# Inverse of the first and last recurrence in one piece, products of r behind it

## The chip, the cores and the metric

The kernel runs on one core of a Trainium2 chip. Its time is device microseconds of one execution; runs are compared by their medians. TensorE (PE) multiplies into PSUM, VectorE (DVE), ScalarE (ACT) and GpSimd (POOL) do the elementwise work, and SyncE (SP) issues the loads.

## The reference, cut to what matters

Two blocks follow each other, all in fp32 on 256 tokens of 1024 features. The first block has two layers over two streams, x and a context ctx. Each layer projects a stream, runs a convolution of 31 taps on one half and a recurrence (RWKV-7 like) on the other, mixes them, and adds a gated FFN:

```python
def step(s, inp):                       # per token, head and direction
    r_t, k_t, v_t, w_t, kk_t, b_t = inp
    sa = -jnp.einsum("bhvk,bhk->bhv", s, kk_t)
    s = s * w_t + sa[..., None] * b_t + v_t[..., None] * k_t   # shapes cut
    y = jnp.einsum("bhvk,bhk->bhv", s, r_t) if emit else None
    return s, y
...
z = val * jax.nn.sigmoid(gate)          # the convolution beside it
z = dwconv(z, conv_w) + conv_b          # 31 taps
z = silu(group_norm(z, CONV_GROUPS, cnorm_g, cnorm_b, LN_EPS))
...
mod_x = silu_c @ ada_w[l] + ada_b[l]    # adaLN: six vectors of 1024 per layer and stream
```

There are 8 heads of 64 and two directions. The second block (FFN, gated mixer, FFN, twice) isn't touched by the change.

## The kernel before, in words

**Recurrences.** `rwkv` (L763) does one stream in chunks of 64 tokens. It makes decays, learning rates and keys, then for each of four pairs of heads the tiles AR (a and r) and BK (k and b), and the 64x64 lower triangles of products of a and b (L862 to L864). `inverse` (L941) inverts these triangles: a transpose on VectorE (L950), 31 steps of two dependent VectorE instructions each (L959, L961: a product of 31-k by k+1 elements, and a subtraction), then two more transposes (L964, L966), matmuls of 32x32 and copies into the tiles Q. It is a generator that is left once behind the 31 steps, so the code emitted there stands between the steps and the rest of the inverse. `reads` (L1011) makes, for one pair of heads, the masked products of r with k and b (VectorE mask L1026), and token-major k and b (transposes L1032, ScalarE copies L1033). `values` (L1038) makes, for two pairs, token-major v (transposes L1049, copies L1051) and the masked products of a and k with it (mask L1062). `chain` (L1072) then goes through the chunks, for two groups of two pairs side by side: a product with Q, the state product (L1104), and the output products.

It runs four times: ctx of layer 0 and x of layer 1 in mode "wide", x of layer 0 in mode "half", and ctx of layer 1 in mode "all". The two wide ones are the first and the last recurrence; in the trace they begin their inverse at 110.0 and 1200.6 us. "half" does reads and values between the chains, "all" without r products.

**What runs beside a wide recurrence.** `wide` (L1402) hands `rwkv` a `fill` that emits steps of other work between the chains' steps: the convolution's input product `conv_in` (L657: eight weight tiles, each loaded, copied to an upper part by ScalarE at L339, its lower part made by VectorE at L340, then 24 matmuls; a product with a sigmoid on VectorE at L668), and then the adaLN vectors 2 to 5 (`ada_steps`, L476: unsplit weight tiles against the conditioning, a small VectorE add at L501). Behind the recurrence it emits the convolution's taps (`conv`, L698: on VectorE at L723, on GpSimd at L729 and L730, a few products on ScalarE at L727).

**What sets the order.** All loops are unrolled. A planner takes the instructions with their dependencies and puts each engine's in a fixed order, by a time line that it simulates: of what is ready, the one that was emitted first goes first; `later(n)` lets what it holds give way to n instructions behind it (the last tiles of the recurrence's own input product, v and gate, are such). Whatever is ready can go into a pause of earlier work. `tc.issue_after(ins)` ties what is emitted inside, on the engine of `ins`, behind `ins` in that engine's order; it adds no wait for its end.

**Shared space.** Tiles of one tag are handed out in program order. In a wide recurrence `reads` and `values` share two PSUM banks, acc10 and acc11 (lane "t"), which one chain group uses later; the input products and adaLN share two banks "pb" (lane "b"); the weight loads four tiles "raw". The token-major v tiles (L1043) come from the tag "xf", whose four tiles hold the normalised input of the block until its last reader, the convolution's input product, is done.

Of the kernel before, what the change touches and what calls it, by code (L numbers as in the profile page):

```python
# [21 lines left out]
ALPHA = 4.0 ** 0.25  # L22
# [5 lines left out]
# weight stream: buffers of raw tiles, of their upper and lower parts, and those the second block adds; the tiles after  # L28
# a norm that are split ahead of it
# [3 lines left out]
# steps of a down product that are cut by tokens at its end, in the first block and in the second  # L33
NLAST = 2, 4
# taps of the convolution on Pool, and on Pool with the products on ACT: first wide stream, second, beside the FFN
NPOOL, NPOOLE, NPOOLC = (14, 3), (12, 4), (30, 0)
NTAP = 2
# adaLN vectors: with the first wide recurrence, with the second, in the first FFN (a step every EVERY tiles)
QB, QE, QC, EVERY = (2, 3, 4, 5), (2, 3, 4, 5), (1,), 2
# steps of the filler per step of the recurrence's chain; instructions that low-priority work gives way to  # L40
FILL = 6
LATER = 1500
# slots of 4 KB in the first block; its norms with the weight tiles behind them held back
# [4 lines left out]
# ---------------------------------------------------------------- host layout  # L48
# [58 lines left out]
# the constants of the first norm  # L107
NCONST1 = CONST["tri0"][0]
LEVELS = (64, 32, 16, 8, 4, 2, 1)
# order of the RWKV column tiles in the weight stream: decay|iclr, k, r, v, gate  # L110
# [3 lines left out]
def _constants():  # L114
# [33 lines left out]
    # level indicators: [b0 level 128 | 64 | 32 | ... | 1 | b1 level 128]  # L148
# [10 lines left out]
    # hindT rows 0..3 for the four heads of 128  # L159
# [6 lines left out]
def _layout(a):  # L166
    f = {}
# [39 lines left out]
    for l in range(2):  # L207
# [27 lines left out]
        f[f"mf{l}"] = (_up(np.concatenate([w[:, 512:1024], w[:, :512]], 1)))  # zf, zq  # L235
        f[f"mt{l}"] = (np.concatenate(
            [w[:, o : o + 512].reshape(4, 2, P, 512).transpose(0, 2, 1, 3).reshape(4, P, D) for o in (1024, 2560)], 0))
        f[f"mg{l}"] = (_up(np.concatenate([w[:, 1536:2048], w[:, 2048:2560]], 1)))  # zg, zu
# [8 lines left out]
# ---------------------------------------------------------------- the program  # L247
# [9 lines left out]
class Prog:  # L257
# [17 lines left out]
    # Tiles of one tag are handed out in program order, so work that runs side by side has tags of its own:  # L275
    # lane "r" (the recurrences), "b" (the large products), "c" (the convolution).
# [33 lines left out]
    @contextlib.contextmanager  # L310
    def later(self, n):
        """what is emitted inside gives way to the n instructions behind it"""
        self.tc.cur_priority += n
        yield
        self.tc.cur_priority -= n

# [25 lines left out]
    # ---- weight stream: tiles of [128, 1024]  # L342
# [6 lines left out]
    def wsplit(self, r):  # L349
        """(hi, lo)"""  # L350
# [7 lines left out]
        if not self.hold:  # L358
            self.split(r, hi, lo)
        elif self.since < NFIRST:  # L360
            # ready ahead of the norm before the product, out of the way of it
            self.nc.scalar.copy(hi, r)  # L362
            self.nc.gpsimd.tensor_sub(lo, r, hi.bitcast(F32))  # L363
        else:
            with self.tc.issue_after(self.hold[0]), self.tc.issue_after(self.hold[1]):
                self.split(r, hi, lo)
            if self.since > NFIRST + 3:
                self.hold, self.since = None, 0
# [7 lines left out]
    # ---- norms  # L376
    def rstd_of(self, ssum, scale, eps, shape):
        """1 / sqrt(ssum * scale + eps)"""
# [7 lines left out]
    def ln_norm(self, x, b, pre):  # L386
        """pre(b, h): what makes half h of the block"""
# [19 lines left out]
    def rms_blocks(self, blocks, keep=False):  # L407
        """the two blocks [128, 1024] of tokens normalised, with keep in place"""
# [17 lines left out]
    def feature_major(self, yb, scale, bias, perm=False, new=None, acc=True):  # L426
        """the two blocks [128, 1024] of tokens, times scale(f) plus bias(f) -> list of 8 (hi, lo) [128, 256]"""
# [4 lines left out]
        # in the banks of the product before, or else two features at a time  # L432
# [4 lines left out]
        # evacuated by ACT and DVE in turns of two, as the products take them; each engine in the order given here  # L437
# [33 lines left out]
    # ---- adaLN  # L471
# [4 lines left out]
    def ada_steps(self, l, qs):  # L476
        """a generator of a quarter of a modulation vector at a time"""
# [31 lines left out]
    def gate_row(self, l, q, v):  # L509
        """[128, 1024]: modulation vector q of stream v in every row"""  # L510
# [11 lines left out]
    # ---- products  # L522
    def up(self, out, w, x, n=NF):
        """out[128, 256] += w tile [128, n*128] (hi, lo) . x list of (hi, lo)"""
# [7 lines left out]
    def down(self, acc, h, w, start, stop, parts=((0, 0), (0, 1), (1, 0), (1, 1))):  # L532
        """acc[b][n] += h[:, b*128..].T @ w[:, n*512..] for the (b, n) of parts"""
# [9 lines left out]
    def down_last(self, acc, args):  # L543
        """the last steps of down: the first half of the tokens is ready early, and of the second the first half
        of the features"""
# [14 lines left out]
    def ffn(self, xf, un, dn, half):  # L560
# [5 lines left out]
        for m in range(NH):  # L566
            self.tick()
            wg, wu = next(us), next(us)
            if m == 0:
                # as the parts of x come  # L570
# [26 lines left out]
    def sqrt_table(self, after):  # L597
        """has the activation table of the norm that follows loaded ahead of it"""
# [21 lines left out]
    # ---- first block: input products  # L620
    def shift(self, l, i, pv, dst, n=P):
        """three-tap convolution along tokens of pv (PSUM [n, 256]) into dst"""
# [7 lines left out]
    def w_in(self, l, x, need, lane=None):  # L630
        """a generator: (slabs of r, k, v, the tile of decay|iclr, the slab of the gate), then after decay|iclr and k,
        after r, and at the end"""
# [24 lines left out]
    def conv_in(self, l, x, z):  # L657
        """a generator: val * sigmoid(gate) into the slab z [128, 4, 256]"""
# [26 lines left out]
    def mixed_in(self, conv, y, perm=False):  # L685
        """the two slabs split into mix tiles, tokens back in their own order"""
# [11 lines left out]
    def conv(self, l, z, acc, npool, hold=False):  # L698
        """31 taps on the slab z [128, 4, 256], group norm and silu, into acc; npool: the numbers of taps
        on Pool, and on Pool with the products on ACT; the others on DVE"""  # L700
# [5 lines left out]
        # taps in the order they are done: one of each kind in turn  # L706
# [35 lines left out]
    def group_norm(self, ys, g, b, eps, func, put=None):  # L742
        """ys: 4 tiles [128, 256], groups of 64 channels on partitions; put(f, func(normed * g + b))"""
# [18 lines left out]
    # ---- RWKV  # L762
    def rwkv(self, l, win, s0, emit, mode, fill=lambda n=1: None):  # L763
        """one stream of 256 tokens, a generator. win: w_in; fill emits a step of what comes beside it. s0: list per two pairs of heads of [128, 2, 2, 64] states or None.
        Sets self.states and, with emit, self.y: the output [128, 4, 256]. mode: all pairs of heads at once ("wide": in
        the tiles of other tags as well) or "half" of them."""
# [7 lines left out]
        # decay, token-major  # L774
# [14 lines left out]
        # in-context learning rate, into the slots of k  # L789
# [8 lines left out]
        # kk  # L798
# [29 lines left out]
        for p in range(4):  # L828
# [7 lines left out]
            # per chunk [1 | direction 0 (64) | direction 1 (64) | 1]  # L836
# [36 lines left out]
        if emit:  # L873
            # sigmoid of the gate's low rank, and per head sum r k r_k
# [16 lines left out]
        if not half:  # L891
            for p in range(len(KB), 4):
                self.reads(p, AR[p], BK[p], emit, GR, KB)
            for g in range(2):
                tok.append(self.values(g, u, AR, BK, wide))
        for _ in inv:
            pass
        Q = self.Q
# [24 lines left out]
        if emit:  # L923
# [3 lines left out]
            def put(f, y):  # L927
                # (normed + (sum r k r_k) v) * g
# [12 lines left out]
    def inverse(self, Ld, Lo):  # L941
        """Unit lower triangular 64x64 matrices j = (direction, pair, chunk), rows on 64 partitions; Ld: their 32x32
        diagonal blocks (only the strict lower part is read), Lo: the block below the diagonal (upper 32 partitions).
        Sets Q, per direction the left operand [128, 16, 64] that applies the inverses: for direction 0 the
        transposed inverse, for direction 1 the inverse."""
# [671 lines left out]
```

## Time and profile before

| | |
|---|---|
| time, median of 3 runs | 2882.7 us (2878.88 to 2889.99) |
| span of the profiled execution | 2888.7 us; the page gives nothing around it |
| TensorE busy | 2715.6 us, 94% of the span |
| VectorE busy | 1746.8 us, 60% |
| ScalarE, GpSimd busy | 1332.2 us, 727.7 us |
| DMA | 430.70 MB, mean 149 GB/s |

The profile is of one execution of the kernel. A TensorE that is shown as busy isn't at its peak, since its clock can be granted at half; the clock is in the table of stretches and in a line of the page.

### The profile page before, as it was taken

To read this page: it belongs to the slowest core of one execution; us is meant where nothing else is said; L and a number is where in the kernel's file an instruction comes from. 1 tells how busy PE (TensorE), PEld (TensorE's weight loads), DVE (VectorE), ACT (ScalarE), POOL (GpSimd) and SP (SyncE) were. 2 spreads that over 40 slices of the span, in tenths; PEclk is the share of its full clock that TensorE was granted. 3 is DMA by queue.
4 is the path that set the end of the run, shared out by engine and by line. 5 is a ranking of instruction groups with operands and counts; after the bars stand their busy time and mean duration, and the time that the engine had idled before them with its cause. 6 is when DMAs were issued, how large, how long until landed. Compare 5 with 4: busy or idle time off the path is not lost. (4 is left out here: it accounts for less than half of the span.)

```text
span 2888.7 us, 53742 instructions
## 1 busy us (share of the span) xinstructions
PE 2715.6 (94%) x22376; PEld 2349.8 (81%) x22376; DVE 1746.8 (60%) x2659; ACT 1332.2 (46%) x2019; POOL 727.7 (25%) x690
## 2 busy tenths in 40 slices
PE   7889989999989998889899899899999999899998
PEld 4866867888668897867699899789899898789897
DVE  3884779634568455874555655665655655665655
ACT  5522554423456345522544544554444444644443
POOL 0385899920130001375200100210200200200200
PEclk9979999999899998979899999999999999999999
DMA  6334424324322344243255555424555555425553
GB/s 241 110 135 145 149 96 175 133 102 143 135 74 103 118 174 155 91 154 132 80 180 185 183 192 188 165 102 139 170 188 184 174 183 173 160 81 179 186 188 118
DMA packets 118768, 430.70 MB, mean 149 GB/s; under 512 B 13175, under 2 KB 13687, under 8 KB 118525
## 3 DMA queue, kind: packets, MB, share of 16 engines
q1 hardware_dynamic: 118524, 427.28, 42.5%
q8 instruction: 175, 2.87, 0.4%
q14 instruction: 69, 0.56, 0.1%
HBM read 425.13 MB, written 2.10 MB: 148 GB/s over the span
## 5 line engine op out<-in xcount | busy, mean ns | idle before, releaser
L340 DVE TENSOR_TENSOR wl<-raw,wh 128x1024 fp32r<-128x1024 f32 (+1 forms) x654 | 847.8, 1299 | 631.0 <-ACT wh L339 405.3
L339 ACT CAST wh<-raw 128x1024 fp32r<-128x1024 f32 (+1 forms) x654 | 682.3, 1046 | 910.2 <-PE pb L331 359.9
L331 PE MATMUL pb<-xf,wh 128*128 128x256 f32 (+1 forms) x2560 | 492.0, 291 | 13.6 <-ACT T1b L582 4.2
L331 PE MATMUL pb<-S,wh 128*128 128x256 f32 x2560 | 493.7, 290 | 5.1 <-DVE wa L628 2.1
L331 PEld LDWEIGHTS pb<-xf,wh 128*128 128x128 f32 (+1 forms) x2560 | 413.3, 196 | 29.0 <-ACT T1b L582 4.6
L331 PEld LDWEIGHTS pb<-S,wh 128*128 128x128 f32 x2560 | 411.4, 193 | 21.8 <-issue 12.0
L331 PE MATMUL ps<-S,wh 128*128 128x256 f32 x2048 | 396.7, 290 | 3.4 <-DVE S L460 2.2
L363 POOL TENSOR_TENSOR wl<-raw,wh 128x1024 fp32r<-128x1024 f32 x22 | 54.1, 2470 | 1336.6 <-ACT wh L362 948.0
L331 PE MATMUL pb<-xf,wl 128*128 128x256 f32 (+1 forms) x1280 | 372.2, 291 | 7.2 <-DVE wl L340 7.2
L331 PE MATMUL pb<-S,wl 128*128 128x256 f32 x1280 | 369.1, 288 | 3.9 <-DVE wl L340 3.9
L331 PEld LDWEIGHTS ps<-S,wh 128*128 128x128 f32 x2048 | 332.8, 195 | 13.1 <-issue 3.7
L331 PE MATMUL ps<-S,wl 128*128 128x256 f32 x1024 | 297.1, 290 | 5.6 <-DVE wl L340 5.6
L331 PEld LDWEIGHTS pb<-xf,wl 128*128 128x128 f32 (+1 forms) x1280 | 249.9, 195 | 14.7 <-DVE wl L340 9.1
L331 PEld LDWEIGHTS pb<-S,wl 128*128 128x128 f32 x1280 | 247.0, 193 | 8.1 <-DVE wl L340 4.7
L331 PE MATMUL acc<-wh,T 128*128 128x512 f32 x704 | 206.3, 393 | 2.4 <-ACT T L339 2.4
L331 PEld LDWEIGHTS ps<-S,wl 128*128 128x128 f32 x1024 | 199.7, 195 | 8.0 <-DVE wl L340 6.4
L331 PE MATMUL acc<-wh,T1b 128*128 128x512 f32 x528 | 160.0, 400 | 3.5 <-ACT T1b L339 3.5
L729 POOL TENSOR_SCALAR tap<-z,cols 128x255 f32<-128x255 f32 (+14 forms) x120 | 149.3, 1253 | 0.0
L331 PEld LDWEIGHTS acc<-wh,T 128*128 128x128 f32 x704 | 127.2, 189 | 26.8 <-ACT T L339 3.0
L729 POOL TENSOR_SCALAR tap<-x,cols 128x246 f32<-128x246 f32 (+6 forms) x104 | 110.6, 1071 | 47.0 <-DVE x L668 46.7
L730 POOL TENSOR_TENSOR x<-x,tap 128x247 f32<-128x247 f32 (+8 forms) x132 | 103.8, 787 | 66.0 <-ACT tap L727 60.0
L331 PEld LDWEIGHTS acc<-wh,T1b 128*128 128x128 f32 x528 | 95.5, 191 | 22.6 <-ACT T1b L339 4.4
(445 smaller groups left out, 4179.0 us busy)
## 6 DMA issues: line engine op xcount, KB each, us to landing
raw<-in_fu SPq DMA_DIRECT2D x132, 512.0 KB, 3.2
raw<-in_ada SPq DMA_DIRECT2D x96, 512.0 KB, 4.1
raw<-in_pu SPq DMA_DIRECT2D x88, 512.0 KB, 3.3
raw<-in_qu SPq DMA_DIRECT2D x88, 512.0 KB, 3.6
raw<-in_fd SPq DMA_DIRECT2D x66, 512.0 KB, 3.2
raw<-in_wr SPq DMA_DIRECT2D x51, 512.0 KB, 3.4
raw<-in_pd SPq DMA_DIRECT2D x44, 512.0 KB, 3.3
raw<-in_qd SPq DMA_DIRECT2D x44, 512.0 KB, 3.3
```

What stands on the lines that cost most here:

```text
L331: return self.nc.tensor.matmul(out, lhsT, rhs, start=start, stop=stop, **kw)
L339: self.nc.scalar.copy(hi, src)
L340: self.nc.vector.tensor_sub(lo, src, hi.bitcast(F32))
L363: self.nc.gpsimd.tensor_sub(lo, r, hi.bitcast(F32))
L729: nc.gpsimd.tensor_scalar(t[:, d], z[:, f, s], w(j), None, ALU.mult)
L730: nc.gpsimd.tensor_add(zc[f][:, d], zc[f][:, d], t[:, d])
```

## The change

`inverse` keeps its last subtraction as `self.inverted`, and a new context `behind` ties VectorE's work to it. In the wide mode the values, all that `fill` emits, and the convolution's taps are traced inside it, so VectorE's instructions of these stand behind the inverse's 31 steps in its queue. The r products (`reads`) are emitted behind the whole inverse instead of ahead of the values, in the modes "wide" and "all". The filler's order changes: the first adaLN vector (2) now comes ahead of the convolution's input product, the others behind it. The rest of the diff takes comments away.

```diff
+    def behind(self, wide=True):
+        return self.tc.issue_after(self.inverted) if wide else contextlib.nullcontext()
...
         next(inv)
         tok = []
         if not half:
-            for p in range(len(KB), 4):
-                self.reads(p, AR[p], BK[p], emit, GR, KB)
-            for g in range(2):
-                tok.append(self.values(g, u, AR, BK, wide))
+            with self.behind(wide):
+                for g in range(2):
+                    tok.append(self.values(g, u, AR, BK, wide))
         for _ in inv:
             pass
+        if not half:
+            for p in range(4):
+                self.reads(p, AR[p], BK[p], emit, GR, KB)
...
-            nc.vector.tensor_sub(X[:, k + 1 : 32, 0 : k + 1], X[:, k + 1 : 32, 0 : k + 1], tv)
+            last = nc.vector.tensor_sub(X[:, k + 1 : 32, 0 : k + 1], X[:, k + 1 : 32, 0 : k + 1], tv)
+        self.inverted = last.ins
         yield
...
-                steps = itertools.chain(self.conv_in(l, x, fl(self.x[0])), self.ada_steps(l, ada))
+                steps = itertools.chain(self.ada_steps(l, ada[:1]), self.conv_in(l, x, fl(self.x[0])),
+                                        self.ada_steps(l, ada[1:]))
...
-                    for _ in range(n):
-                        next(steps, None)
+                    with self.behind():
+                        for _ in range(n):
+                            next(steps, None)
...
-            drain(self.conv(l, fl(self.x[0]), fl(self.x[1]), (NPOOL, NPOOLE)[l]))
+            with self.behind():
+                drain(self.conv(l, fl(self.x[0]), fl(self.x[1]), (NPOOL, NPOOLE)[l]))
```

## Rows read from the trace of the kernel before

**Rows 1.** The page: span, and the TensorE clock granted in 40 slices, in tenths.
```profile
span 2888.7 us, 53742 instructions
...
PEclk9979999999899998979899999999999999999999
```
**Rows 2.** Windows (stretch: length, busy us of each engine, clock, DMA), first wide recurrence.
```profile
110.03:186.42 76.39, 65.62 (x684) 50.75 (x685) 70.38 (x156) 28.85 (x52) 46.14 (x46) 0.91 0.44 153
186.42:219.70 33.28, 32.85 (x455) 23.45 (x453) 21.40 (x35) 11.71 (x18) 27.63 (x33) 0.59 0.20 70
219.70:281.80 62.10, 62.10 (x693) 42.11 (x693) 24.14 (x53) 17.20 (x37) 34.65 (x42) 0.92 0.46 159
```
**Rows 3.** The same for the last recurrence; columns PE, PEld, DVE, ACT, POOL.
```profile
1200.55:1274.70 74.15, 63.59 (x666) 50.04 (x669) 71.11 (x153) 23.95 (x41) 46.17 (x47) 0.90 0.41 143
1274.70:1317.40 42.70, 42.28 (x568) 27.58 (x560) 23.47 (x42) 14.75 (x24) 28.22 (x34) 0.66 0.41 151
1317.40:1371.00 53.60, 53.49 (x656) 40.49 (x656) 22.17 (x53) 12.14 (x24) 26.97 (x34) 1.00 0.32 118
```
**Rows 4.** Groups of VectorE, 110.03 to 189.4 us: busy us, mean ns, idle before.
```profile
L723 DVE SCALAR_TENSOR_TENSOR T1c<-x,cols,T1c 128x255 f32<-128x255 f32 (+6 forms) x39 | 24.4, 635 | 0.0
L959 DVE TENSOR_TENSOR T<-S,S 128x31 f32<-128x31 f32 (+15 forms) x31 | 12.7, 410 | 0.2
L961 DVE TENSOR_TENSOR S<-S,T 128x31 f32<-128x31 f32 (+15 forms) x31 | 12.5, 405 | 0.2
L340 DVE TENSOR_TENSOR wl<-raw,wh 128x1024 fp32r<-128x1024 f32 x8 | 11.3, 1411 | 0.2 <-PE pb L331 0.2
L1026 DVE TENSOR_TENSOR S<-acc,const 128x256 f32<-128x256 f32 x16 | 6.1, 407 | 0.0
```
**Rows 5.** Timeline of VectorE in the first inverse: start us, duration us, instruction.
```profile
113.30 0.22 DVE L959 TENSOR_TENSOR T<-S,S 128x60 f32<-128x60 f32 x1
113.55 0.22 DVE L961 TENSOR_TENSOR S<-S,T 128x60 f32<-128x60 f32 x1
...
129.46 0.39 DVE L959 TENSOR_TENSOR T<-S,S 128x231 f32<-128x231 f32 x1
129.88 0.40 DVE L961 TENSOR_TENSOR S<-S,T 128x231 f32<-128x231 f32 x1
...
148.76 0.94 DVE L959 TENSOR_TENSOR T<-S,S 128x255 f32<-128x255 f32 x1
```
**Rows 6.** Timeline of TensorE, convolution input product, at either clock.
```profile
121.73 0.41 PE L331 MATMUL pb<-xf,wl 128*128 128x256 f32 x1
...
122.37 0.41 PE L331 MATMUL pb<-xf,wl 128*128 128x256 f32 x1
...
128.45 0.28 PE L331 MATMUL pb<-xf,wl 128*128 128x256 f32 x1
...
128.81 0.28 PE L331 MATMUL pb<-xf,wl 128*128 128x256 f32 x1
```
**Rows 7.** Timeline of TensorE: last convolution input matmul; values' transposes of pairs 1, 2, 4.
```profile
158.06 0.28 PE L331 MATMUL pb<-xf,wl 128*128 128x256 f32 x1
...
171.15 0.63 PE L1049 MATMUL acc<-const,S 128*64 128x128 f32 x4
...
179.89 0.52 PE L1049 MATMUL acc<-const,S 128*64 128x128 f32 x3
...
204.55 0.63 PE L1049 MATMUL acc<-const,S 128*64 128x128 f32 x2
```
**Rows 8.** Groups of GpSimd in the last recurrence, 1219 to 1353 us.
```profile
L729 POOL TENSOR_SCALAR tap<-x,cols 128x246 f32<-128x246 f32 (+5 forms) x48 | 50.7, 1062 | 23.0 <-DVE x L668 22.8
L730 POOL TENSOR_TENSOR x<-x,tap 128x246 f32<-128x246 f32 (+5 forms) x64 | 49.9, 781 | 28.3 <-ACT tap L727 25.1
```
**Rows 9.** Groups of TensorE: adaLN matmuls in both chain stretches, the last recurrence's second.
```profile
L331 PE MATMUL pb<-raw,csil 128*32 128x512 f32 x52 | 14.1, 746 | 0.0
...
L331 PE MATMUL pb<-raw,csil 128*32 128x512 f32 x23 | 4.6, 603 | 0.0
```

## The prediction

> **What bounds the kernel now.** I read the page first. TensorE is busy almost throughout; the places where that breaks, and where the granted clock sags, are in the two wide recurrences: slices 3 and 18 of the clock line are its lowest [rows 1]. Then I cut both wide recurrences into three stretches by VectorE's and TensorE's timelines: the inverse (from its first transpose, L950, to the transpose behind its last subtraction, L964), the stretch up to the first state product of the chains (L1104), and the chains. The inverse takes 76.4 and 74.2 us, VectorE is busy in nearly all of it, and TensorE is idle for 10.8 and 10.6 us of it [rows 2, 3]. The stretch behind it has TensorE full, at 0.59 and 0.66 of the clock; the chains have it full at 0.92 and 1.00. So the inverse stretch is bound by VectorE, all behind it by TensorE or by hand-overs that TensorE's record hides.
>
> The groups of VectorE in the first inverse tell why it is long: its 62 dependent instructions have only 25.2 us in 79 us; the rest is convolution taps (24.4), weight splits (11.3) and r masks (6.1) [rows 4]. The timeline shows how they get in: where nothing else is ready, one step follows the other at 0.25 us for 60 elements and at 0.42 us for 231; else a tap or a split of 1.2 us stands between any two. Once GpSimd runs its taps, a step of 255 elements takes 0.94 us [rows 5].
>
> **The change part by part.** I follow one path through each wide recurrence: inverse, convolution inputs, values, two pairs of r products, chains.
>
> *Inverse in one piece.* The step widths (32-a)a, a = 1 to 31, sum to 5456, a mean of 176. Between the two steps of rows 5, 0.25 us at 60 and 0.42 us at 231, that is 0.37 us; 62 of them make 23. With the first transpose (some 2: the second pair of steps starts 3.3 us into the stretch [rows 2, 5]) and what stays untied (the two gate tiles' splits and shifts, and in the first recurrence the norm of x: some 4, estimated from a split's 1.4 and a shift's 0.5) it is 29 us. GpSimd is idle meanwhile, since its taps need the tied product of L668. So the inverse ends near 139 and 1229 us of the trace, 47 and 45 us sooner [rows 2, 3]. Bounds: above, the 25.2 us of the steps as they ran, some beside GpSimd; below, the 0.25 us step throughout, 15.5: 22 to 33 with the rest.
>
> *What is tied.* That time isn't saved; it moves. The convolution's input product (L657: 8 tiles, 192 matmuls) needs a split from VectorE for each tile, and all splits are now behind the inverse. At the full clock three matmuls take 0.36 us [rows 6], 23 us in all. Before, it ran under the inverse and was over at 158 us [rows 7]. Now it starts behind the L964 and L966 transposes and the first split, some 5 us after the inverse, and ends near 139+5+23+2 = 169, and 1259 in the last recurrence. It also holds up the values: their token-major tiles (L1043) take over the four slots of the block's normalised input, which that product reads to its end. In the trace of before nothing shows that wait, since the r products kept the two banks even longer: the values' first transposes start at 171, 13 us after the last of the input product [rows 7].
>
> *Values.* Four pairs, 8.7 us for the first and 11.1 us on average [rows 7], the later ones at the sunken clock. I take 9.5, as nearer to the first, which ran beside a full VectorE: 38 us, until 207 and 1297. Bounds: 8.7, and 12.3, the mean of the last two [rows 7].
>
> *r products behind.* They share the two banks with the values, so now they follow. Before, they needed no place on the path; now the first two pairs stand on it, since a chain's state product needs their k and b. Their sixteen masks have 6.1 us [rows 4]; per pair 1.5 us of masks and about as much again for matmuls and for copies, each waiting for the other in two banks: some 6 us, 12 for two. Bounds: 3 (masks and matmuls alone) and 15 a pair, the pace at which four of them took the time from the inverse's start at 110 to the values' at 171 [rows 2, 7]. First state products: near 219 and 1309, against 219.7 and 1317.4.
>
> *adaLN vector 2 moved ahead of the convolution inputs.* It needs no split, so it and the gate tiles are TensorE's work under the inverse. Its eight loads now go ahead of the eight convolution tiles on SP's queue; the convolution tiles have the whole inverse to land in, and the DMA engines are busy for 0.44 and 0.41 of it [rows 2, 3]. Its two small adds wait behind the inverse, and with them two banks "pb", for which the convolution inputs wait: that is in the 5 us above. Off the path otherwise. The other vectors follow the convolution inputs, and come under the values and r products. So the chains no longer share TensorE with adaLN matmuls: of those the chain stretches hold 14.1 and 4.6 us [rows 9]. The other two pairs of r products come in, with 4.
>
> *Chains.* 62.1-14.1+4 = 52 and 53.6-4.6+4 = 53 us: ends near 271 and 1362 against 281.8 and 1371. In the first recurrence TensorE has other work behind and beside the chains (the norm and the next stream's products), so nothing is lost: 10 us. In the last one nothing is left to fill with, and the convolution's norm needs the taps on GpSimd: 50.7+49.9 us of them [rows 8], which start with the first convolution product, now near 1241 instead of 1219.8. Without a hole they end at 1342; with the 28.3 us of holes that they had, at 1370. With half the holes they end before the chains, with all of them 8 us behind. I take 8 us of the 9.
>
> *The other two recurrences.* "half" is unchanged. "all" has its k and b transposes behind the inverse, untied; TensorE there has the other stream's FFN to do: 0.
>
> Sum: 10+8 = 18 us. The profiled execution has a span of 2888.7 us [rows 1], 6.0 above the median of the runs, 2882.7, and inside their 2878.9 to 2890.0; I take the 18 us from the median: **2865 us**.
>
> [...]
>
> **The rivals.**
> *A. The hole is paid back (about 2880 us).* TensorE's work doesn't shrink. Under the 29 us of the inverse the changed kernel can give it the gate tiles (two of 24 matmuls, 6 us), one adaLN vector (32 instructions of the kind of rows 9, 9 us) and the first value transposes (some 3 us with what surrounds them). So 11 us of new idle stand against 10.8 us of old idle [rows 2], and a few us at the lower clock behind it take the rest. For it: TensorE is full after the inverse. Against: the old idle and a sunken clock behind it were as large. Each recurrence then gains 0 to 3 us: 2877 to 2883.
> *B. The two banks decide (about 2912 us).* Values and r products hand over between three engines with two banks; if VectorE's order puts taps and splits between them, values take 12.3 us and r products 15 us a pair. Then the first state products come near 169+49+30 = 248 and 1338, the chains end near 300 and 1391, 18 and 20 us late; of the first some is filled with the next stream's products: +22 to +38 in all. The sign turns where values and two pairs together take more than 60 us instead of 50. For it: the taps, splits and masks of rows 4, 42 us, now all stand behind the inverse. Against: the taps come last in program order.
> [...]
> *D. The tie does nothing:* the planner orders by its own time line, so a step might find its order already. Against: in every inverse of the trace other work stands between the steps; I give it no chance of its own.
>
> **How the numbers follow.** Forecast 0.50 (2850 to 2874), A 0.22, B 0.18, C 0.10. The range, 2842 to 2898, takes in the forecast, A, half of C and a little of B. Half a per cent, 14.4 us, is about what a measurement of this kernel can tell from no change: four fifths of the forecast and all of C lie beyond it, 0.50; slower by more than that is most of B, 0.14; the rest is 0.36.
>
> **What would show it.** Right: an inverse of 25 to 33 us with nothing but gate and norm work in it; L340 of the convolution inputs all behind it; the values' first copies after the last of these; r masks after the values; chains without adaLN matmuls; the last recurrence's chains end 5 to 12 us sooner. Wrong: other tied work still between the steps; r products at more than 10 us a pair; convolution inputs at 0.64 us per three matmuls; GpSimd's taps in the last recurrence ending behind the chains.

## The result: 1.4 per cent slower, and the profile after

The changed kernel takes 2926.7 us (median of 4 runs, 2918.7 to 2929.9) against 2886.3 us of the kernel before beside it on the same chip: a ratio of 1.0143, 95% interval 1.012 to 1.0165. The prediction was 2865 us with a range up to 2898, so it was wrong in sign. Lines of the changed kernel stand 4 to 7 further down than those of before (L331 is L335, L340 is L344, L668 is L672, L950 is L956, L964 is L971, L1026 is L1033, L1062 is L1069).

The page of the changed kernel: span, TensorE's busy time, its busy tenths and its clock in 40 slices, to be read against [rows 1].

```profile
span 2928.1 us, 53744 instructions
...
PE 2737.7 (93%) x22376; PEld 2374.9 (81%) x22376; DVE 1741.0 (59%) x2659; ACT 1330.0 (45%) x2017; POOL 724.3 (25%) x690
...
PE   7799998999989998889999899899999999899998
...
PEclk8887998999999999978899999999999999999999
```

Before, the same page has TensorE busy for 2715.6 us in a span of 2888.7. The 22376 matmuls are the same in number, and the span is 39.4 us longer: 22.1 us because they took longer, 17.3 us because TensorE stood idle longer (190.4 against 173.1). VectorE, whose work the change rearranged, is busy for no longer than before. The mean granted clock of the two profiles is 0.939 now and 0.946 before; at these means some 23 us more of the span are lost to the clock (an estimate, 0.061 of 2928.1 us less 0.054 of 2888.7), about what the matmuls took longer. Each profile is of one execution.

Windows of the kernel before, cut at the four starts of an inverse and at a point 1288.7 us before the end (stretch: length, busy us of PE, PEld, DVE, ACT, POOL, granted clock, DMA share, GB/s).

```profile
0.00:110.03 110.03, 89.54 (x921) 65.35 (x922) 58.97 (x105) 58.13 (x106) 18.12 (x34) 0.94 0.54 194
110.03:450.40 340.37, 311.19 (x3126) 242.28 (x3126) 238.44 (x414) 154.51 (x267) 259.74 (x270) 0.90 0.37 130
450.40:870.30 419.90, 402.22 (x3685) 329.12 (x3683) 247.11 (x388) 180.38 (x289) 177.81 (x169) 0.93 0.36 126
870.30:1200.55 330.25, 309.76 (x3069) 276.89 (x3068) 208.57 (x328) 165.04 (x261) 26.94 (x30) 0.96 0.38 132
1200.55:1600.00 399.45, 375.21 (x3235) 308.63 (x3235) 239.23 (x406) 158.75 (x247) 118.32 (x130) 0.91 0.41 144
```

The same windows of the changed kernel.

```profile
0.00:114.56 114.56, 92.73 (x909) 67.84 (x910) 59.15 (x106) 57.63 (x106) 19.78 (x36) 0.91 0.54 190
114.56:475.30 360.74, 322.08 (x3140) 255.78 (x3139) 231.08 (x412) 152.51 (x265) 250.73 (x259) 0.87 0.35 121
475.30:897.80 422.50, 402.72 (x3682) 331.73 (x3680) 247.24 (x390) 179.99 (x290) 183.91 (x178) 0.93 0.36 125
897.80:1222.50 324.70, 307.12 (x3051) 275.64 (x3050) 207.46 (x328) 164.69 (x258) 28.26 (x32) 0.97 0.39 134
1222.50:1639.40 416.90, 385.13 (x3267) 316.21 (x3266) 241.50 (x407) 159.72 (x249) 115.30 (x128) 0.90 0.40 139
```

The loss stands in the two stretches that hold the wide recurrences: 20.4 us in the second window, 17.5 in the fifth. In each of them about half is busy time of TensorE (10.9 and 9.9 us more, at a lower clock) and half is idle time (9.5 and 7.5 us). The fifth also has 32 matmuls more than before, which moved over its edges: some 4 us of the 9.9 (an estimate, at its mean of 0.12 us). Another 4.5 us come ahead of the first inverse, and the two recurrences between give 3.0 back.

Now the cuts of [rows 2, 3] in the changed kernel: inverse, then up to the first state product, then up to the end of the chains.

```profile
114.56:146.23 31.67, 16.87 (x90) 8.92 (x88) 25.74 (x76) 13.51 (x24) 0.00 (x0) 0.72 0.42 151
146.23:232.41 86.18, 82.33 (x980) 61.63 (x980) 56.42 (x99) 31.52 (x51) 56.37 (x62) 0.91 0.62 208
232.41:316.40 83.99, 81.86 (x889) 68.36 (x886) 37.55 (x76) 18.80 (x39) 50.17 (x59) 0.79 0.12 40
1222.50:1249.71 27.21, 16.15 (x95) 8.29 (x93) 24.87 (x69) 7.78 (x13) 0.00 (x0) 0.77 0.45 157
1249.71:1337.50 87.79, 83.27 (x984) 62.23 (x985) 58.45 (x102) 29.13 (x47) 54.09 (x59) 0.86 0.53 187
1337.50:1407.90 70.40, 66.20 (x833) 53.42 (x831) 36.52 (x81) 14.82 (x31) 43.97 (x53) 0.85 0.11 39
```

The inverse did become short, and the sunken stretch behind it (0.59 and 0.66 in [rows 2, 3]) came up to 0.91 and 0.86. But the three add up to 201.8 and 185.4 us from the inverse's start, against 171.8 and 170.5 before. Inverse and second stretch together take 117.9 and 115.0 us (109.7 and 116.9 before). The chains grew more: 84.0 and 70.4 us instead of 62.1 and 53.6, and their clock fell from 0.92 and 1.00 to 0.79 and 0.85. In the first recurrence 9.7 of the 30 us come back behind the chains (158.9 us to the next inverse instead of 168.6), since the next stream's products were already done under them.

### The profile page after: what moved, and what is told of

Same layout as the page of the kernel before. It is cut to its first block, busy times and chain, and to the rows that moved or that the text cites. A ratio compares the mean times of both kernels' runs of the same rounds, so it can differ in the third digit from the quotient of the medians.

```text
span 2928.1 us, 53744 instructions
## 1 busy us (share of the span) xinstructions
PE 2737.7 (93%) x22376; PEld 2374.9 (81%) x22376; DVE 1741.0 (59%) x2659; ACT 1330.0 (45%) x2017; POOL 724.3 (25%) x690
## 5 line engine op out<-in xcount | busy, mean ns | idle before, releaser
L344 DVE TENSOR_TENSOR wl<-raw,wh 128x1024 fp32r<-128x1024 f32 (+1 forms) x654 | 846.1, 1297 | 650.8 <-ACT wh L343 403.0
L335 PE MATMUL pb<-S,wh 128*128 128x256 f32 x2560 | 504.9, 294 | 6.8 <-DVE S L632 4.6
L335 PE MATMUL pb<-xf,wh 128*128 128x256 f32 (+1 forms) x2560 | 497.2, 293 | 8.4 <-DVE T1b L589 4.4
L335 PEld LDWEIGHTS pb<-S,wh 128*128 128x128 f32 x2560 | 419.6, 197 | 25.0 <-issue 14.6
L335 PEld LDWEIGHTS pb<-xf,wh 128*128 128x128 f32 (+1 forms) x2560 | 419.3, 199 | 22.9 <-DVE T1b L589 8.1
L335 PE MATMUL ps<-S,wh 128*128 128x256 f32 x2048 | 395.3, 290 | 3.2 <-DVE S L464 1.8
L335 PE MATMUL pb<-S,wl 128*128 128x256 f32 x1280 | 374.5, 293 | 3.9 <-DVE wl L344 3.9
L335 PE MATMUL pb<-xf,wl 128*128 128x256 f32 (+1 forms) x1280 | 375.4, 294 | 1.5 <-DVE wl L344 1.5
L335 PEld LDWEIGHTS ps<-S,wh 128*128 128x128 f32 x2048 | 331.6, 194 | 12.6 <-issue 3.7
L335 PE MATMUL ps<-S,wl 128*128 128x256 f32 x1024 | 296.2, 289 | 5.3 <-DVE wl L344 5.3
L335 PEld LDWEIGHTS pb<-xf,wl 128*128 128x128 f32 (+1 forms) x1280 | 253.7, 198 | 7.2 <-DVE wl L344 2.1
L335 PEld LDWEIGHTS pb<-S,wl 128*128 128x128 f32 x1280 | 251.9, 197 | 9.3 <-DVE wl L344 4.5
L335 PE MATMUL acc<-wh,T 128*128 128x512 f32 x704 | 206.3, 393 | 1.7 <-ACT T L343 1.7
L335 PEld LDWEIGHTS ps<-S,wl 128*128 128x128 f32 x1024 | 198.9, 194 | 8.0 <-DVE wl L344 6.5
L335 PE MATMUL acc<-wh,T1b 128*128 128x512 f32 x528 | 159.5, 400 | 3.5 <-ACT T1b L343 3.5
L335 PEld LDWEIGHTS acc<-wh,T 128*128 128x128 f32 x704 | 127.3, 189 | 26.0 <-ACT T L343 2.1
L335 PEld LDWEIGHTS acc<-wh,T1b 128*128 128x128 f32 x528 | 95.2, 191 | 22.4 <-ACT T1b L343 4.4
```

The lines of the kernel that those rows point to most:

```text
L335: return self.nc.tensor.matmul(out, lhsT, rhs, start=start, stop=stop, **kw)
L344: self.nc.vector.tensor_sub(lo, src, hi.bitcast(F32))
```

## The experiments

Seventeen kernels, each timed against the kernel before on the same chip. "Tie" is the `behind` around values, filler (convolution inputs and adaLN) and convolution taps; "reads" is the emission of the r products behind the inverse; "order" is adaLN vector 2 ahead of the convolution inputs. Busy and idle are TensorE's, in each kernel's one profile, less those of before; a profiled execution can stand some us off its kernel's median (e6 and e7 lie 11 and 10 us under theirs, e13 lies 14 above).

| kernel | ratio, 95% interval | busy | idle |
|---|---|---|---|
| changed kernel (tie, reads, order) | 1.0143, 1.012 to 1.0165 | +22.1 | +17.3 |
| e1 reads, order | 1.0061, 1.0036 to 1.0086 | +8.6 | -0.7 |
| e2 tie, order | 1.0062, 1.0043 to 1.008 | +18.7 | -5.3 |
| e3 tie, reads | 1.0213, 1.0195 to 1.0232 | +12.4 | +42.0 |
| e4 tie | 1.0108, 1.0085 to 1.013 | +25.4 | +7.1 |
| e5 changed, filler untied | 1.0185, 1.0167 to 1.0204 | +34.5 | +8.3 |
| e6 order | 1.0073, 1.0049 to 1.0098 | -2.2 | +2.8 |
| e7 reads | 1.0093, 1.0067 to 1.0118 | -4.3 | +15.1 |
| e8 taps tied, order | 0.9951, 0.9934 to 0.9969 | -24.8 | -0.4 |
| e9 changed, values untied | 1.0145, 1.011 to 1.0181 | +19.1 | +25.9 |
| e10 taps tied | 1.0059, 1.0035 to 1.0084 | +10.7 | +7.9 |
| e11 changed, two vectors ahead | 1.0109, 1.0078 to 1.0139 | +20.9 | +7.0 |
| e12 before, vectors 2 and 3 exchanged | 1.0054, 1.0036 to 1.0072 | +9.3 | +3.0 |
| e13 e8 with reads in the last recurrence | 1.0004, 0.9984 to 1.0024 | +5.1 | +4.8 |
| e14 e8 with two vectors ahead | 1.0103, 1.0069 to 1.0136 | +6.5 | +14.5 |
| e15 before, vectors 4 and 5 exchanged | 1.0010, 0.9993 to 1.0028 | -5.3 | +5.9 |
| e16 changed, 4 and 5 exchanged | 1.0168, 1.0123 to 1.0212 | +25.6 | +20.4 |
| e17 e8, 4 and 5 exchanged | 0.9936, 0.9909 to 0.9964 | -24.3 | -3.5 |

**One part undone, or the tie alone (e1 to e4).** Theory 1 is that the tie costs, theory 2 the r products, theory 3 the filler's order.

```diff
e1:  -with self.behind(wide):   # around values
     -with self.behind():       # around the filler's step, and around conv
e2:  +if not half: for p in range(4): self.reads(...)   # ahead of the values again
e3:  -chain(ada_steps(l, ada[:1]), conv_in(...), ada_steps(l, ada[1:]))
     +chain(conv_in(...), ada_steps(l, ada))
e4:  both of e2 and e3
```

e1: 

> The changed kernel without the tie: the values', the filler's and the convolution's VectorE work is free to run between the steps of the inverse again; the products of r stay behind the inverse and adaLN vector 2 stays ahead of the convolution inputs. Theory 1 (the tie costs: TensorE has no work for the inverse and 192 matmuls of the convolution inputs land on the path behind it): close to the kernel before, 2880 to 2895 us, inverse again over 60 us long. Theory 2 (the products of r on the path cost): no better than 2915. Theory 3 (the order of the filler costs, since it takes the adaLN matmuls from under the chains, where TensorE then sinks to the lower clock): 2905 to 2920.

e2: 

> The changed kernel with the products of r emitted ahead of the values again, untied; tie and filler order as changed. Theory 1: 2915 to 2930, since the convolution inputs still stand behind the inverse. Theory 2: from the last mask of the values to the first state product the changed kernel takes 21 and 27 us; with the products of r back under the inverse these go, against some 8 us more of inverse in each: 2890 to 2900. Theory 3: 2915 to 2930.

e3: 

> The changed kernel with the filler's old order (convolution inputs first, all four adaLN vectors behind them); tie and products of r as changed. Theory 1: 2920 to 2935 (the inverse loses even the adaLN matmuls that TensorE had in it). Theory 2: no change, 2920 to 2930. Theory 3: adaLN matmuls stand under the chains again and keep TensorE at the upper clock there: 2900 to 2915.

e4: 

> The kernel before with the tie alone: products of r ahead of the values, old order of the filler. Theory 1: the loss is nearly all there, 2915 to 2930. Theory 2: the loss is gone, 2880 to 2895. Theory 3: the loss is gone or small, 2885 to 2905.

Taking the tie away wins back 0.82 per cent, some 24 us, and moving the r products ahead as much; neither theory holds alone. As a price for the whole kernel theory 3 falls: the new order saves 20 us in this kernel, since without it TensorE has next to nothing to do under the inverse. Windows of the two inverses of e3:

```profile
111.80:147.20 35.40, 8.26 (x56) 7.12 (x56) 28.02 (x75) 13.86 (x23) 0.00 (x0) 0.60 0.05 15
1237.90:1268.50 30.60, 8.65 (x62) 7.60 (x61) 27.27 (x71) 5.63 (x9) 0.00 (x0) 0.67 0.02 5
```

TensorE is idle for 27 and 22 us there, where the changed kernel has 15 and 11, and the page has 24.7 us more idle time. e2 puts a price on the r products. Its three stretches, and its last chains:

```profile
111.90:149.40 37.50, 30.76 (x365) 21.50 (x364) 30.19 (x92) 17.69 (x33) 0.00 (x0) 0.86 0.41 141
149.40:215.79 66.39, 63.56 (x681) 48.47 (x681) 43.38 (x70) 20.68 (x32) 36.28 (x37) 0.77 0.41 144
215.79:290.60 74.81, 74.59 (x813) 55.07 (x811) 39.25 (x84) 21.24 (x44) 62.02 (x72) 0.86 0.36 128
...
1311.10:1383.70 72.60, 71.83 (x817) 50.83 (x816) 34.27 (x76) 18.15 (x36) 57.18 (x70) 0.91 0.37 131
```

With the r products back under the inverse TensorE has 31 us of work in it instead of 17, and the first chains end 178.7 us after the inverse's start instead of 201.8. The inverse is only 6 us longer for it. The r products were work that filled the inverse, not work in its way.

**Parts of the tie, and single parts alone (e5 to e8).**

```diff
e5:  changed kernel, -with self.behind(): around the filler's step only
e6:  kernel before, filler in the new order
e7:  kernel before, +for p in range(4): self.reads(...) behind the inverse
e8:  e6, +with self.behind(): around conv (the taps) only
```

e5: 

> The changed kernel with the convolution inputs and adaLN untied, so that their splits run between the inverse's steps; values and convolution taps stay tied, products of r behind, new order. If the part of the tie that costs is the one on the convolution inputs (TensorE without work in the inverse, the inputs on the path), nearly all that taking the whole tie away gave comes back: 2895 to 2905. If it is the taps and values that must not be late: 2915 to 2930.

e6: 

> The kernel before with the new filler order alone (adaLN vector 2 ahead of the convolution inputs). With the tie the new order gained 0.46 per cent, with tie and late products of r 0.7. If it gains because it gives TensorE work in a short inverse, it is worth nothing here, where the inverse has work: 2878 to 2890. If it gains because it moves adaLN to the values' stretch or spreads it, it gains here too: 2865 to 2875.

e7: 

> The kernel before with the products of r behind the inverse alone. With the tie they cost 0.8 (new order) and 1.05 per cent (old order). If their price is the stretch between the values and the first state product, whatever the inverse does: 2900 to 2912. If they cost only because the tie has left everything else behind the inverse too: 2880 to 2892.

e8: 

> The kernel before with the convolution's taps alone tied behind the inverse, and the new filler order; products of r ahead, convolution inputs and values free. The inverse loses 24 us of taps and stays at some 50 us, TensorE keeps its work in it. If the inverse's end is on the path of the kernel before, the first state product comes 10 us sooner in each recurrence: 2862 to 2875. If the path goes through the convolution inputs, the values and TensorE, and the inverse has slack: 2878 to 2892, and a late end of the taps on GpSimd shows as some us more.

e5 is a miss for theory 1: with the convolution inputs free under the inverse, and over 13 and 16 us sooner after its start, the kernel is slower still, 1.0185. The end of the convolution inputs isn't what sets the time, and neither is the hole in the inverse alone: TensorE is idle for only 6.7 and 4.5 us of e5's two inverses. The order alone and the r products alone lose 0.7 and 0.9 per cent. e8 gains where its parts don't: it takes 24 us of taps out of the inverse and leaves TensorE its work there.

```profile
109.30:154.60 45.30, 41.18 (x462) 31.82 (x462) 38.21 (x100) 23.02 (x40) 5.85 (x7) 0.92 0.50 166
154.60:208.92 54.32, 48.28 (x608) 35.49 (x607) 40.82 (x74) 16.48 (x28) 52.51 (x52) 0.81 0.44 153
208.92:282.20 73.28, 67.24 (x801) 49.84 (x800) 36.53 (x75) 22.07 (x45) 62.99 (x74) 0.90 0.37 131
1192.30:1237.80 45.50, 41.74 (x474) 32.79 (x473) 42.11 (x103) 17.76 (x29) 8.71 (x8) 0.92 0.44 152
1237.80:1281.05 43.25, 41.92 (x607) 31.80 (x606) 38.31 (x69) 17.04 (x28) 39.61 (x44) 0.88 0.53 185
1281.05:1346.00 64.95, 64.01 (x805) 46.51 (x804) 34.24 (x75) 17.14 (x34) 49.57 (x62) 1.00 0.34 122
```

TensorE is idle for 4 us in each inverse, where before had 11 in a longer one. In the last recurrence the chains end 153.7 us after the inverse's start, 17 us sooner than before, at a clock of 0.88 and 1.00 behind the inverse. In the first (172.9 us) nothing is gained. By its row of the table e8's whole gain is shorter busy time (-24.8) and none of it idle time (-0.4); why its clock was higher (0.954 in its profile, 0.946 in that of before) isn't shown.

**Rival causes (e9 to e11).**

```diff
e9:   changed kernel, -with self.behind(wide): around values
e10:  kernel before, +with self.behind(): around conv only
e11:  changed kernel, adaLN untied, ada[:2] ahead of conv_in; conv_in still tied
```

e9: 

> The changed kernel with the values untied: their masks may stand between the inverse's steps; convolution inputs, adaLN and taps stay tied, products of r behind, new order. In the changed kernel TensorE waits 8.8 and 7.2 us at the end of the inverse for a mask of the values, with other work behind it in its order. Theory 4 (the tie on the values blocks TensorE's queue): 2900 to 2912. Theory 1 (the tie on the convolution inputs, for which the values wait anyway): no change, 2918 to 2932.

e10: 

> The kernel before with nothing but the convolution's taps tied behind the inverse: old filler order, products of r ahead. With the new order this was 0.5 per cent faster than before, and the new order alone 0.7 slower. If the two add up, the taps' tie alone gives 1.2 per cent: 2843 to 2855. If the new order is what fills the shortened inverse: 2875 to 2892.

e11: 

> The changed kernel with two adaLN vectors ahead of the convolution inputs instead of one, and adaLN's own VectorE adds untied, so that their banks come free within the inverse; all else as changed. TensorE gets about 9 us more work for the 15 and 11 us in which it was idle in the two inverses. If the hole in the inverse costs its length: 10 to 18 us less, 2908 to 2918. If it costs nothing because the path behind it is hand-overs of values and products of r: 2920 to 2930.

Theory 4 falls: with the masks free the ratio is the same, and the two inverses still hold 13.5 and 13.8 us of idle time. e11 leans to the hole: 8 us more work in each inverse, 10 us less in all, its lower forecast; but its interval and the changed kernel's overlap, so that isn't shown, and e5, with a small hole and a longer time, speaks against it. e10 shows that the parts don't add: the taps' tie alone loses 0.6 per cent and the order alone 0.7, and together they gain 0.5.

**What any other order costs (e12 to e17).** Whether the small losses of single parts mean anything was asked of controls: two adaLN vectors exchanged, the same work a little differently ordered. e13 and e14 tried to carry e8 further.

```diff
e12:  -QB, QE = (2, 3, 4, 5), (2, 3, 4, 5)
      +QB, QE = (3, 2, 4, 5), (3, 2, 4, 5)
e15, e16, e17:  (2, 3, 5, 4) in the kernel before, the changed one, e8
e13:  e8, reads behind the inverse where l == 1
e14:  e8, ada[:2] ahead of conv_in
```

e12: 

> A control: the kernel before with adaLN vectors 2 and 3 exchanged in the filler of both wide recurrences, so that the same work runs in a slightly other order and nothing is longer or later. If every new order costs 0.6 to 1 per cent, as undoing single parts suggests, whatever it is meant to do (the clock falls in other places): 2895 to 2912. If the parts have costs of their own: 2878 to 2890.

e13: 

> The kernel with taps tied and new filler order (0.5 per cent faster than before), and the products of r behind the inverse in the last recurrence alone. Products of r alone behind the inverse made the last recurrence's chains end 10 us sooner and the first one's 30 us later. If that gain adds: 2852 to 2862. If the products of r stand on the path whenever the inverse is short, as in the changed kernel: 2872 to 2885.

e14: 

> The kernel with taps tied and the new filler order, but with two adaLN vectors ahead of the convolution inputs instead of one. If adaLN in the inverse is what makes that kernel fast: 2850 to 2862. If the convolution inputs, then later by some 9 us, hold up values and taps: 2870 to 2885.

e15: 

> A second control: the kernel before with adaLN vectors 4 and 5 exchanged in the filler. The first control (2 and 3) was 0.54 per cent slower. If the order of before is one that fits by chance or by choice and any other costs: again 0.4 to 0.9 per cent, 2896 to 2910. If vector 2 was simply needed early: no change, 2880 to 2892.

e16: 

> The same exchange of vectors 4 and 5 in the changed kernel. If the changed kernel has already lost the fitting order, another one may go either way, by up to 0.5 per cent: 2912 to 2940. If its loss is all structure: 2922 to 2930.

e17: 

> The same exchange in the kernel with taps tied and new filler order, which was 0.5 per cent faster than before. If its gain is structure (a shorter inverse that still has TensorE's work): 2862 to 2874. If it is an order that happens to fit: 2876 to 2895.

The exchange of 4 and 5 leaves all three kernels where they were: 1.0010, 1.0168 with an interval that meets the changed kernel's, 0.9936. But it hardly is another order. Compared by the tiles that its matmuls read and write, TensorE's order in the trace differs at 10 of the 22376 places in e15, at 66 in e16, at 85 in e17, and at 4498 in e12. So e15 to e17 show that the results repeat, and not what another order costs. The exchange of 2 and 3 does reorder, and costs 0.54 per cent with the same work. So a single loss of that size (e1, e2, e10) can't be laid to the part that was changed, and neither can e8's gain of 0.5. The changed kernel's 1.4 per cent is well above it. The 0.8 that e1 and e2 win back is above it too, but one such control gives no spread. e13 and e14 lose e8's gain.

Nine of the seventeen came out outside every range that was set down for them: e1, e3, e4, e5, e6, e9, e10, e13 and e14 (e4, e9 and e13 by less than 2 us).

What one profile says of a stretch needs care. The last chains of e16 and then of e12:

```profile
1337.55:1417.60 80.05, 77.65 (x834) 62.36 (x832) 35.43 (x82) 14.74 (x31) 43.84 (x53) 0.68 0.10 34
```

```profile
1321.58:1385.90 64.32, 64.32 (x662) 45.23 (x658) 20.13 (x49) 11.77 (x23) 20.35 (x27) 0.84 0.37 132
```

From 1263 us of the changed kernel's trace to 1691, e16's TensorE runs the same matmuls in the same order. Still they took 77.7 us here at 0.68 (834 recorded), and 66.2 at 0.85 in the changed kernel (833). So these 11.5 us are no price of an order. Whole executions differ in the same way: the ten of e13 go from 2880.7 us at a mean granted clock of 0.953 to 2901.5 at 0.942. e12 has 662 matmuls against 656 in [rows 3], 11 us longer at 0.84 instead of 1.00, with 5.5 us more in adaLN matmuls; from one profile it isn't shown that this is its loss.

## Why the prediction was wrong, step by step

**Right: the inverse in one piece.** 31.7 and 27.2 us against 29. Groups of VectorE in it, for [rows 4]:

```profile
L965 DVE TENSOR_TENSOR T<-S,S 128x31 f32<-128x31 f32 (+15 forms) x31 | 10.6, 342 | 1.0
L967 DVE TENSOR_TENSOR S<-S,T 128x31 f32<-128x31 f32 (+15 forms) x31 | 10.6, 342 | 1.0
```

21.2 us for the 62 steps, where 23 were worked out. With GpSimd idle a step of 255 elements took 0.42 or 0.43 us. In the kernel before, with GpSimd in its taps, one took 0.41 us (at 139.41 us) and another 0.94 [rows 5], so it isn't 0.94 whenever the taps run. TensorE was idle for 14.8 and 11.1 us, where rival A said 11. Right too: adaLN's matmuls against weights left the chains, values started behind the convolution inputs, r masks behind the values, and from the first copy of values to the first r mask it took 40 us in either recurrence (38 forecast). GpSimd's taps ended 13 us ahead of the last chains.

**Too small: what lies between the inverse and the convolution inputs.** Their last matmul ended 66 us after the inverse's start in either recurrence, not 59, and the last VectorE product behind them (L672) began at 70. VectorE's timeline behind the first inverse (start, length, instruction) shows what the prediction left out.

```profile
147.38 1.91 DVE L973 STREAM_TRANSPOSE S<-S 128x1024 f32<-128x1024 f32 x1
149.22 2.32 DVE L344 TENSOR_TENSOR wl<-raw,wh 128x1024 fp32r<-128x1024 f32 x2
...
152.28 2.48 DVE L999 COPY S<-S 32x512 f32<-32x512 f32 x4
154.79 0.68 DVE L987 COPY S<-ps 32x512 f32<-32x512 f32 x1
155.40 0.67 DVE L987 COPY S<-acc 32x512 f32<-32x512 f32 x1
158.46 0.68 DVE L1015 TENSOR_SCALAR S<-acc 32x512 f32<-32x512 f32 x1 [2.40 <-PE acc L335]
160.08 0.68 DVE L1015 TENSOR_SCALAR S<-ps 32x512 f32<-32x512 f32 x1 [0.93 <-PE ps L335]
160.79 1.23 DVE L344 TENSOR_TENSOR wl<-raw,wh 128x1024 fp32r<-128x1024 f32 x1
```

The inverse has a second half (off-diagonal blocks): copies and two products in turn, 9 us between the second split and the third, and 256 small matmuls of TensorE's, 8.3 us, between those of the inputs. Before, both lay under the values. The r products gave some of that back: from their first mask to the first state product it took 10 and 9 us instead of 12. That product came 86 and 88 us after the inverse instead of 80.

**The step that failed: "Chains", 52 and 53 us.** They measured 84.0 and 70.4. The prediction took before's stretch, struck out adaLN's 14.1 and 4.6 us, and added 4 for r products. Two things were wrong in it.

*The r products were priced at 4 us and took 12.0 and 15.0 of TensorE's time there.* They are emitted ahead of the chains and so come first, but only one of the four pairs was done before the first state product: 24 of the 32 transposes (L1039) and 180 and 179 of the small matmuls stand in the chains, where the prediction had two pairs. These rows of TensorE, the first recurrence's two and then the last one's, overlap with other matmuls (180 of 224 ns would be 40.3 us one after the other, and 7.5 us of them count as busy):

```profile
L335 PE MATMUL acc<-S,S 64*64 64x64 f32 x180 | 7.5, 224 | 0.5 <-DVE S L1033 0.5
L1039 PE MATMUL acc<-const,S 128*128 128x128 f32 x24 | 4.5, 327 | 0.8 <-DVE S L1033 0.8
...
L335 PE MATMUL acc<-S,S 64*64 64x64 f32 x179 | 9.5, 283 | 1.2 <-DVE S L1033 1.2
L1039 PE MATMUL acc<-const,S 128*128 128x128 f32 x24 | 5.5, 381 | 0.8 <-DVE S L1033 0.8
```

Their masks (L1033), the first state updates (L1118, L1115), in either recurrence:

```profile
L1033 DVE TENSOR_TENSOR S<-acc,const x16: 407/424/426, 222.2 to 246.9; 128x256 f32<-128x256 f32 x16
...
L1118 DVE TENSOR_TENSOR st<-acc,pc x2: 408/416/424, 239.2 to 257.1; 128x256 f32<-128x256 f32 x2
```

```profile
L1033 DVE TENSOR_TENSOR S<-acc,const x16: 407/424/425, 1328.4 to 1361.2; 128x256 f32<-128x256 f32 x16
...
L1115 DVE TENSOR_TENSOR st<-acc,st x8: 409/424/426, 1353.3 to 1404.3; 128x256 f32<-128x256 f32 x8
```

The masks of four pairs take 25 and 33 us, 6 to 8 a pair as forecast; but the chains' first state product, begun at 232.4 and 1337.5, was through only at 239.2 and 1353.3, since TensorE did its parts between theirs. e2 against the changed kernel prices the r products at 0.81 per cent.

*The clock didn't stay.* The chains were priced at 0.92 and 1.00 and ran at 0.79 and 0.85. In the last recurrence, 66.2 us of matmuls at 0.85 would be 56 at full clock if all their time went by it. The pair of e16 and the changed kernel says rather 58: the clock took 25.6 us from e16's stretch (0.32 of 80.05) and 10.6 from this one (0.15 of 70.40), and the 15 us between them made 11.5 us of matmuls, so 10.6 make some 8 (an estimate). So of the 17 us over the forecast 8 to 10 are clock, 4 are idle time, and 3 to 5 are more work of TensorE's. In the first, the stretch also took in 39.8 us of the next stream's products (3.3 before), of which the 9.7 us came back:

```profile
L335 PE MATMUL pb<-S,wh 128*128 128x256 f32 x85 | 24.6, 373 | 0.5 <-DVE S L464 0.5
...
L335 PE MATMUL pb<-S,wl 128*128 128x256 f32 x42 | 15.2, 368 | 0.0
```

The new order took adaLN out of the chains and put 96 of its matmuls, 20.5 us, into the stretch ahead of them, where the clock rose; it fell in the chains. What makes it fall there isn't settled. Of the windows of chains of all these kernels, twelve hold no adaLN matmul against weights (first recurrence: changed, e1, e5, e9, e11, e16; last: changed, e5, e9, e11, e13, e16), and they show 0.68 to 0.85; those that hold some show 0.77 to 1.00. In the last recurrence e1 and e7, with r products behind and 12 and 16 such matmuls in the chains, show 0.97. e1's chains, the first without any and the last with 12:

```profile
222.58:301.10 78.52, 77.38 (x870) 64.09 (x868) 34.85 (x72) 18.30 (x39) 47.95 (x58) 0.80 0.10 35
...
1316.76:1380.20 63.44, 62.61 (x847) 48.68 (x844) 29.09 (x67) 14.78 (x30) 29.67 (x38) 0.97 0.20 68
```

So the new order may have cost the chains their clock. No run took these matmuls alone out of the chains, and e4's last chains hold 86 of them at 0.77.

**The clock of the convolution inputs.** In the first recurrence three of their matmuls took 0.64 us from 152 to 155 us of the trace and 0.36 from there on; the granted clock was 0.50 from 150 to 155 us and 1.00 from 155 to 160. In the last they took 0.64 from 1256 to 1260 and from 1264.5 to 1267.7. At 0.28 us more for three that is some 1 and 3 us (estimates). So 0.64 us for three, one of the signs that were to show the prediction wrong, was there, and cost little. A lower clock also stands where the record has no idle time: e12's last chains ran at 0.84 with TensorE busy for 64.32 of 64.32 us.

**The rivals.** B came nearest: slower, 2912 us, chains ending near 300 and 1391 (316 and 1408 measured). Its mechanism, slow values and 15 us for a pair of r products, wasn't there. A's hole was there (14.8 and 11.1 us), but it didn't set the time. C, near 2840 us, was a TensorE at work and at a higher clock behind the inverse. The clock there did rise, from 0.59 and 0.66 to 0.91 and 0.86, and the kernel was 1.4 per cent slower; no run shows what this rise alone is worth. D is out.

**The deeper error** is the sum itself. It followed one path, inverse to chains, and counted as gained what left the path. But TensorE is busy for 93 or 94 of 100 us in either kernel, its matmuls are the same, and the time is their length at the granted clock plus TensorE's holes. By that account the change could gain only by a higher clock or by smaller holes, and both came out worse. Of what was taken out of the inverse, putting the r products back won 0.81 per cent (e2) and putting the convolution inputs back won nothing (e5); how the loss divides between clock and holes is read from one execution of each kernel.

## What to carry to other kernels

Where one engine is full, ask of each moved piece what that engine does in its place, and price a stretch by all the work that engine gets there, at a clock that may change with it (here from 0.59 and 0.66 to 0.91 and 0.86 behind the inverse, from 0.92 and 1.00 to 0.79 and 0.85 in the chains). Leave under a dependent chain the work that can fill the full engine: here the r products, 0.81 per cent. Moving out what that engine doesn't run (here the taps) is worth a try; with a little adaLN work moved in it was 0.5 per cent faster, but without that it was 0.6 slower, so the order had as much to say as the tie. Before half a per cent is laid to a part, time several reorderings of the same work and compare their instruction orders: here one cost 0.54 per cent, and another, which cost nothing, had left the order almost as it was.

## What the runs showed of the hardware

The same 22376 matmuls kept TensorE busy for 2690.8 us (e8) to 2750.1 us (e5), 59 us apart, where idle time differed by 47 (167.8 in e2, 215.1 in e3). Not all of that is the kernels' doing: ten executions of e13 differ by 21 us, with mean granted clocks from 0.942 to 0.953. A full TensorE isn't a TensorE at full clock: in the kernel before it was busy for all of the 20 us from 195 to 215 us, at a granted clock of 0.50, and the same matmuls of the last chains in the same order took 66.2 us at 0.85 and 77.7 at 0.68, with 4.2 and 2.4 us of idle time among them.
